# A hybrid decoder block on one core: the output projection and the second norm join the interleaved order of the mixers

## The chip, the core and the metric

The kernel runs on one core of a Trainium2 chip, whose engines each take their own instructions in order: TensorE (PE) for matrix products, VectorE (DVE), ScalarE (ACT) and GpSimd (POOL) for the rest, and SyncE (SP), whose queue starts most of the transfers. The metric is the device time of one execution in microseconds; lower is better. The granted clock is that of TensorE as a share of its full speed.

## What is computed

One decoder block for a sequence of 512 rows of width 1024. The part that the change touches, cut from the reference:

```python
h = rms_norm(x, norm1_w[l]) * (1.0 + scale1) + shift1
proj = h @ w_in[l]
aq, ak, av, gq, gk, gv, gg, glr = jnp.split(proj, split_points, axis=-1)
att = sliding_window_attention(aq..., ak..., av..., attn_sinks[l])
go = gla_chunked(gq..., gk..., gv..., log_a...)
go = rms_norm(go, gla_norm_w[l]).reshape(B, S, GLA_V_W) * jax.nn.silu(gg)
mixed = jnp.concatenate([att, go], axis=-1) @ w_out[l]
x = x + gate1 * mixed
h2 = rms_norm(x, norm2_w[l]) * (1.0 + scale2) + shift2
x = x + gate2 * peer_ffn(h2, peer_wq[l], peer_subkeys[l], peer_u[l], peer_v[l])
return rms_norm(x, final_norm_w)
```

The expert retrieval `peer_ffn` multiplies `h2` by `wq`, takes the best 16 keys twice, and works with rows of `u` and `v`; it makes up the time after about 258 us and its code is not touched.

## The kernel before

The 512 rows are four blocks of 128, `n` = 0 to 3. Products of float32 accuracy are made from two halves: a value is split into a high part (`hi`, `his`, `ah`, `gh`, `h2Th`, copied by ACT) and the rest (`lo`, `los`, `al`, `gl`, `h2Tl`, subtracted by DVE), and `mm3` (L119) adds three matmuls: high by high (L120), low by high (L121), high by low (L122).

Up to about 78 us the kernel computes the norm, the first modulations and narrow projections. Then comes a stretch in which five kinds of work are woven together by hand-written generators: the two wide products `pn` with `w_v` (`wide_load`, `wide_part`, tiles `wv..`; the results are `gv` and `gg`), attention (`sc` scores, `pt` transposes, `PT`, `po`), gated linear attention (`pa` scores of many tiny matmuls, `pd`, `go`), the sums of modulations 3 and 4 (`macc3`, `macc4`, then `mt3`, `mt4`, eight one-column matmuls each), and the gates. A class `Weave` decides the order: each step says which engine it needs, for how long by a written estimate, which places of a ring it takes and which marks must have been set, and the class gives the engine that is free first the step with the highest urgency. The order is then fixed for PE, ACT, DVE, SP and POOL alike (`manual_schedule`).

Behind that, outside the woven part, `mixers(n0)` runs for blocks 0 and 1 and then for 2 and 3, in an order that the framework's scheduler decides. For each half `q` of the 1024 columns it loads two pieces of 1 MB of `w_out` (`wo`), splits each in two parts (`his`, `los` of 128x1024, in a ring of four slots shared with the later splits of `wq` and `u`), and forms `pw` for two blocks. `mg` = `pw` times the gate (L1148), `x` + `mg` (L1149), the sum of squares (L1150). `second_norm` (L1154) takes the root (`rb..`), scales (`xs`, L1173 on ACT and L1175 on DVE), transposes (`x2t`, L1177), applies the modulation (`h`, L1181 on DVE, L1184 on ACT) and splits into `h2Th` (ACT, L1186) and `h2Tl` (DVE, L1187). Raw weights (`wo`, `wa` of the modulations, `wv`, `wq`, `u`) come through one pool of three slots of 1 MB, filled by SP's queue in order. Then `pq`, the products with `wq`, begin: `pq00` and `pq01` are the two halves of retrieval head 0, `pq10` and `pq11` those of head 1, first for blocks 0 and 1 (24 matmuls of 256 columns each), then, with the same names, for blocks 2 and 3; `qsc` copies the results.

## Time and profile before

| | |
|---|---|
| median of 3 runs | 1439.2 us (1437.43 to 1441.88) |
| the profiled execution | 1442.22 us, its span 1440.4 us |
| PE busy | 1396.3 us, 97% of the span |
| DVE busy | 1272.8 us, 88% |
| ACT busy | 669.0 us, 46% |
| POOL busy | 611.7 us, 42% |
| mean granted clock | 0.989 |
| HBM read | 399.71 MB |

The span is from the first to the last instruction, the time of the execution a little more. Busy time of an engine is the time in which an instruction of its own is being worked on; for PE the ends of matmuls are modelled, so its busy share says little of how fast it runs. "Idle before" is the time an engine stood still ahead of an instruction, and the name behind it is what ended last of the things waited for.

### The profile page before, as it was taken

How to read it: one execution, taken by the hardware profiler on the slowest of the kernel's cores; microseconds unless marked ns; L12 is line 12 of the kernel's file. 1: busy time of each engine (PE TensorE's matmuls, PEld its weight loads, DVE VectorE, ACT ScalarE, POOL GpSimd, SP SyncE). 2: the span in 40 equal slices, each digit the busy share in tenths (PEclk: the TensorE clock that was granted, in tenths of full speed). 3: DMA queues.
4: the chain of work that ended last, by engine and by line, in shares of the span. 5: the costliest groups of instructions: out<-in, count | busy, mean ns of one | idle time of the engine just before them, and what ended most of it. 6: DMA issues, size and time to landing. Idle time of an engine off the chain costs nothing.

```text
span 1440.4 us, 23298 instructions
## 1 busy us (share of the span) xinstructions
PE 1396.3 (97%) x8788; PEld 1229.5 (85%) x8788; DVE 1272.8 (88%) x2321; ACT 669.0 (46%) x1124; POOL 611.7 (42%) x400
## 2 busy tenths in 40 slices
PE   5999999999999999999989999999999999999997
PEld 4776687888999999999979888888888888888885
DVE  7778867589999999999978999999999898898996
ACT  4557566533344477766863333333233333323333
POOL 2000000144525444333035777677776776555510
PEclk9999999999999999999999999999999999999999
DMA  9621555353358999999889999999999999999962
GB/s 359 245 89 59 205 176 205 105 214 126 111 193 325 387 321 347 348 328 355 291 323 416 412 413 413 410 413 407 394 401 395 403 381 412 391 414 410 411 245 73
DMA packets 129985, 443.81 MB, mean 308 GB/s; under 512 B 11952, under 2 KB 48592, under 8 KB 109520
## 3 DMA queue, kind: packets, MB, share of 16 engines
q1 hardware_dynamic: 71136, 256.40, 47.0%
q0 software_dynamic: 47136, 171.99, 30.5%
q10 hardware_dynamic: 11600, 13.93, 2.7%
q8 instruction: 69, 1.13, 0.3%
q14 instruction: 44, 0.36, 0.1%
HBM read 399.71 MB, written 42.47 MB: 307 GB/s over the span
## 4 chain that ended last, share of the span: by engine, by line
PE 75%; DVE 10%; issue 6%; ACT 3%; DMA 3%; POOL 2%; SPq 0%; ACTq 0%; POOLq 0%; DVEq 0%
PE acc L122 12%; PE acc L120 12%; PE acc L121 12%; PE ph L122 8%; PE ph L120 8%; PE ph L121 8%; POOL spr L1542 2%; PE pg L1463 2%; PE pw L121 1%; PE pw L120 1%; PE pn L120 1%; DVE macc L282 1%; PE pw L122 1%; DMA u<-in_uT_dram 1%; PE pj L120 1%
## 5 line engine op out<-in xcount | busy, mean ns | idle before, releaser
L120 PE MATMUL ph<-h2Th,his 128*128 128x320 f32 x1024 | 320.1, 313 | 2.4 <-ACT his L1905 1.9
L122 PE MATMUL ph<-h2Th,los 128*128 128x320 f32 x1024 | 316.6, 310 | 2.5 <-DVE los L1912 1.8
L121 PE MATMUL ph<-h2Tl,his 128*128 128x320 f32 x1024 | 316.1, 309 | 0.0
L1598 POOL DMA_INDIRECT gu<-in_u_dram,ix_u x128 | 215.4, 1683 | 146.0 <-DVE gu L1608 81.1
L1633 POOL DMA_INDIRECT gv<-in_vP_dram,ix_v x128 | 212.8, 1662 | 111.4 <-DVE gacc L1638 88.4
L120 PEld LDWEIGHTS ph<-h2Th,his 128*128 128x128 f32 x1024 | 193.1, 189 | 4.3 <-ACT his L1905 2.1
L122 PEld LDWEIGHTS ph<-h2Th,los 128*128 128x128 f32 x1024 | 192.8, 189 | 3.5 <-DVE los L1912 2.0
L121 PEld LDWEIGHTS ph<-h2Tl,his 128*128 128x128 f32 x1024 | 193.1, 189 | 0.8
L1542 POOL DMA_INDIRECT spr<-in_u_dram,spix x64 | 104.7, 1636 | 171.5 <-DVE spr L1548 129.2
L120 PE MATMUL acc<-his,Ah 128*128 128x512 f32 x432 | 168.0, 389 | 0.0
L121 PE MATMUL acc<-los,Ah 128*128 128x512 f32 x432 | 168.0, 389 | 0.0
L122 PE MATMUL acc<-his,Al 128*128 128x512 f32 x432 | 168.0, 389 | 0.0
L1638 DVE SCALAR_TENSOR_TENSOR gacc<-gv,hg,gacc 128x1024 f32<-128x1024 f32 x127 | 162.6, 1280 | 2.1 <-DMA gv<-in_vP_dram,ix_v 1.8
L1608 DVE SCALAR_TENSOR_TENSOR gu<-gu,h2n 128x1024 f32<-128x1024 f32 x128 | 155.5, 1219 | 2.7 <-DMA gu<-in_u_dram,ix_u 2.7
L120 PE MATMUL acc<-hi,Ah 128*128 128x512 f32 x336 | 131.3, 391 | 0.0
L122 PE MATMUL acc<-hi,Al 128*128 128x512 f32 x336 | 131.1, 390 | 0.0
L121 PE MATMUL acc<-lo,Ah 128*128 128x512 f32 x336 | 130.7, 389 | 0.0
L1908 ACT ACTIVATE Ah<-gr 128x768 fp32r<-128x768 f32 x64 | 53.5, 836 | 134.5 <-PE acc L121 128.4
L113 ACT ACTIVATE his<-u 128x1024 fp32r<-128x1024 f32 x86 | 90.5, 1054 | 20.7 <-PE ph L121 9.5
L114 DVE TENSOR_TENSOR los<-u,his 128x1024 fp32r<-128x1024 f32 x75 | 91.4, 1222 | 8.6 <-ACT his L113 8.6
L121 PEld LDWEIGHTS acc<-los,Ah 128*128 128x128 f32 x432 | 81.1, 188 | 16.9
L120 PEld LDWEIGHTS acc<-his,Ah 128*128 128x128 f32 x432 | 81.1, 188 | 16.9
(697 smaller groups left out, 2899.8 us busy)
## 6 DMA issues: line engine op xcount, KB each, us to landing
u<-in_uT_dram SPq DMA_DIRECT2D x43, 1024.0 KB
gr<-Gd SPq DMA_DIRECT2D x15, 1536.0 KB
Gd<-gs SPq DMA_DIRECT2D x10, 2048.0 KB
gsp<-ge ACTq DMA_DIRECT2D x40, 320.0 KB
wa<-in_w_ada_dram SPq DMA_DIRECT2D x12, 1024.0 KB
wo<-in_w_out_dram SPq DMA_DIRECT2D x8, 1024.0 KB
wq<-in_wq_dram SPq DMA_DIRECT2D x8, 1024.0 KB
gp<-gsp SPq DMA_DIRECT2D x22, 320.0 KB
```

The lines of the kernel that those rows point to most:

```text
L113: nc.scalar.activation(hi, src, AF.Copy)
L114: lo_eng.tensor_tensor(lo, src, hi, OP.subtract)
L120: nc.tensor.matmul(acc, lh, rh, start=start, stop=False)
L121: nc.tensor.matmul(acc, lh, rl, start=False, stop=False)
L122: return nc.tensor.matmul(acc, ll, rh, start=False, stop=stop)
L1463: nc.tensor.matmul(pt[:, i, :], o12[:, g, 0, :, r], o2[:, g, m, :, r], start=(m == 0), stop=(m == 2))
L1542: nc.gpsimd.indirect_dma_start(out=sp[m], out_offset=None, in_=a["u"], in_offset=bass.IndirectOffsetOnAxis(ap=sp["ix", i][:, j:j + 1], axi ...
L1598: nc.gpsimd.indirect_dma_start(out=ur, out_offset=None, in_=a["u"], in_offset=bass.IndirectOffsetOnAxis(ap=ix_u[:, s:s + 1], axis=0))
L1608: nc.vector.scalar_tensor_tensor(ur, ur, 1.0, h2n, op0=OP.mult, op1=OP.mult, accum_out=hid[:, s:s + 1])
L1633: nc.gpsimd.indirect_dma_start(out=vr, out_offset=None, in_=a["vP"], in_offset=bass.IndirectOffsetOnAxis(ap=ix_v[:, s:s + 1], axis=0))
L1638: nc.vector.scalar_tensor_tensor(gacc, vr, hg[:, s:s + 1], gacc, op0=OP.mult, op1=OP.add)
L1908: nc.scalar.activation(grp(Ah), A, AF.Copy)
```

## The change

`Weave` and all its estimates go. The generators stay, each `yield` now only a place where a step begins, and a table `ORDER` of numbers says which generator takes its next step. The output projection and the second norm become generators of the same part: `pools` (opens the pools of the next stage and loads `x`), `out_load` (loads and splits `w_out` once, the first k row of the first half on its own), `project` (products `pw` of one half and one block), `joined`, `norm_root`, `norm_half`, `norm_end`. All four blocks of a half share the split, and eight PSUM banks take `pw`. `macc3` and `macc4` lie in the tile `Eg`, the transposes `gt` use other banks, and the loads of `wa` stand in another order. The ring of splits starts at 8 for `wq`.

```diff
-class Weave:
...
+ORDER = """
+2 2 2 2 0 0 0 0 2 0 0 0 0 22 2 2 25 25 0 0 2 25 21 25 0 2 25 25 13 13 13 25 2 0 1 13 1 1 2 1 1 1 1 25 2 1 13 1
...
+"""
...
+    def pools():
+        nonlocal h2p, h2Th, h2Tl, h2n, ix_u, ix_v, gg_g, hl, frW
+        yield
+        frA_s.close()
...
+        ring["slots"] = [hl.tile([P, 4, D], FR, name=name) for name in ("his", "los")]
+        yield
+        frT_s.close()
+        frW = frW_s.enter_context(tc.tile_pool(name="frW", bufs=1, side="right", reuse_waits="tile"))
+        for n in range(NT):
+            yield
...
+            nc.sync.dma_start(x1s[n], a["x"][n * P:(n + 1) * P, :])
+
+    def out_load():
+        for i in range(8):
+            q, k = divmod(2 * i, KD)
+            if i % 2 == 0:
+                yield
+                wo = raw([P, 4, 512], f"wo{q}{k}")
+                nc.sync.dma_start(wo, a["w_out"][:, k:k + 4, q * 512:(q + 1) * 512])
+            k0 = i % 2 * 2
...
+            yield
+            hi, lo = (t[:, i % 4].rearrange("p (a b) -> p a b", a=2)[:, :m] for t in ring["slots"])
+            nc.scalar.activation(hi, wo[:, k0:k0 + m, :], AF.Copy)
+            yield
+            nc.vector.tensor_tensor(lo, wo[:, k0:k0 + m, :], hi, OP.subtract)
...
+    def project(q, n, tag):
+        for k in range(KD):
+            yield
+            if k == 0:
+                pw[n, q] = pbank(f"pw{n}{q}") if tag == "ph" else bank(f"pw{n}{q}", tag)
+            h, l = [(ahl[n][i][:, k, :] if k < 4 else ghl[n][i][:, (k - 4) * P:(k - 3) * P]) for i in range(2)]
+            oh, ol = rows[q, k]
+            mm3(pw[n, q], h, l, oh, ol, k == 0, k == KD - 1)
...
+    def norm_half(n, half):
...
+        if half:
+            nc.scalar.activation(xs, x1s[n][:, 512:], AF.Copy, scale=h2s["r", n])
+        else:
+            nc.vector.tensor_scalar(xs, x1s[n][:, :512], h2s["r", n], None, op0=OP.mult)
...
+        for i in range(4):
+            nc.tensor.transpose(pt[:, i, :], xs[:, i * P:(i + 1) * P], ident)
...
+    def norm_end(n):
+        yield
...
+        nc.scalar.activation(h2Th[:, :, n * P:(n + 1) * P], h2s[n], AF.Copy)
+        yield
+        nc.vector.tensor_tensor(h2Tl[:, :, n * P:(n + 1) * P], h2s[n], h2Th[:, :, n * P:(n + 1) * P], OP.subtract)
...
+        parts = ([gla_scores(0), gla_scores(1), wide_load(0), wide_load(1), pools()] + [gla_gate(n) for n in ALL]
...
+                 + [project(0, n, t) for n, t in enumerate(("m", "m", "ph", "ph"))]
+                 + [project(1, n, t) for n, t in enumerate(("pt", "po", "m", "m"))]
+                 + [modulation(3), modulation(4)] + [attention_parts(n) for n in ALL])
+        for part in parts:
+            next(part)
+        for i in ORDER.split():
+            next(parts[int(i)], None)
...
+    hilo.n = 8
...
-    for n in range(0, NT, 2):
-        mixers(n)
```

PE at the start of the woven part, from the first product with `wv00` on; before:

```order
L120 MATMUL pn00_897<-wv00h_835,hTh_186 128x512
L121 MATMUL pn00_897<-wv00l_836,hTh_186 128x512
L122 MATMUL pn00_897<-wv00h_835,hTl_187 128x512
...
L798 MATMUL sc000_904<-am_128,identb_130 128x2x128
...
L884 MATMUL pa1_932<-Eg_113 64x64 x4
L891 MATMUL pa1_932<-Eg_113 64x32 x48
L120 MATMUL pn00_897<-wv02h_879,hTh_186 128x512
```

The same place after the change, from the k-step with which the first scores `sc` are now preceded (`wv02` is the third k-step, `pn01` the second block):

```order
L98 MATMUL pn00_897<-wv02h_829,hTl_187 128x512
L96 MATMUL pn01_898<-wv02h_829,hTh_186 128x512
L97 MATMUL pn01_898<-wv02l_830,hTh_186 128x512
L98 MATMUL pn01_898<-wv02h_829,hTl_187 128x512
...
L759 MATMUL sc000_932<-am_128,identb_130 128x2x128
...
L835 MATMUL pa1_946<-Eg_113 64x64 x4
L842 MATMUL pa1_946<-Eg_113 64x32 x48
L96 MATMUL pn01_898<-wv02h_829,hTh_186 128x512
```

Three k-steps of both blocks (18 matmuls) now stand ahead of `sc00`, where one of block 0 stood (3); 12 wide matmuls lead up to the `pa1` products before and 21 after.

PE where the projection ends, after the change: `pw31` and `pw21` are the second halves of blocks 3 and 2.

```order
L98 MATMUL pw31_2249<-his_1921,gl3_2137 128x512
L1009 MATMUL mt4_2310<-ones_79,Eg_113 128x1 x8
L96 MATMUL pw21_2326<-his_1921,ah2_1793 128x512
L97 MATMUL pw21_2326<-los_1922,ah2_1793 128x512
L98 MATMUL pw21_2326<-his_1921,al2_1792 128x512
L1131 MATMUL x2t0_2332<-ident_73,xs00_2299 128x128 x4
...
L98 MATMUL pw21_2326<-his_1921,gl2_2091 128x512
L1131 MATMUL x2t30_2411<-ident_73,xs30_2408 128x128 x4
L1131 MATMUL x2t31_2418<-ident_73,xs31_2398 128x128 x4
L96 MATMUL pq00_2510<-h2Th_1912,his_1921 128x256
L96 MATMUL pq01_2511<-h2Th_1912,his_1921 128x256
L97 MATMUL pq00_2510<-h2Tl_1913,his_1921 128x256
```

Before, `mt3` and `mt4` stood together ahead of the first `pw`, the transposes of blocks 0 and 1 stood before `pw21` and `pw31` began, and `pq00` followed the last `pw` with the transposes of blocks 2 and 3 behind it.

ACT and DVE at that place after the change, ACT first (from `h` of block 0's end; `h2_123` holds blocks 1 to 3):

```order
L1147 ACTIVATE h2_123_2356<-x2t10_2351,modT_83,aT_84 128x128 x2
L89 ACTIVATE his_1921<-wq0_2503 128x1024
L1154 ACTIVATE h2Th_1912<-h2_0_2337 128x8x128
L1147 ACTIVATE h2_123_2356<-x2t11_2361,modT_83,aT_84 128x128 x2
L89 ACTIVATE his_1921<-wq0_2503 128x1024
L1119 ACTIVATE xs31_2398<-x1_3_2234,rb3y_2339 128x512
L89 ACTIVATE his_1921<-wq1_2663 128x1024 x2
L1154 ACTIVATE h2Th_1912<-h2_123_2356 128x8x128
```

DVE:

```order
L1144 TENSOR_SCALAR h2_123_2356<-x2t11_2361,aT_84,modT_83 128x128 x2
L1121 TENSOR_SCALAR xs30_2408<-x1_3_2234,rb3y_2339 128x512
L1090 TENSOR_TENSOR mg21_2416<-pw21_2326,gate1b_102 128x512
L90 TENSOR_TENSOR los_1922<-wq0_2503,his_1921 128x1024
L90 TENSOR_TENSOR los_1922<-wq1_2663,his_1921 128x1024
L1092 TENSOR_TENSOR x1_2_2221<-x1_2_2221,mg21_2416 128x512
L90 TENSOR_TENSOR los_1922<-wq1_2663,his_1921 128x1024
L1156 TENSOR_TENSOR h2Tl_1913<-h2_123_2356,h2Th_1912 128x8x128
```

The split of `wq` (`his`, `los`) and the ends of the second norm of block 1 (`h2Th`, `h2Tl`) now alternate with the last steps of the projection (`mg21`, `x1_2`), where before `h2Th` and `h2Tl` of blocks 0 and 1 were finished ahead of the split of `wq`. From the first `pq` of blocks 2 and 3 on (the next `pq00` behind `pq11`), every engine has the order that it had.

## Rows read from the trace of the kernel before

**Rows 1.** The page: busy us of each engine (share of the span, instructions), and part 4, the chain of work that ended last, by engine.
```profile
PE 1396.3 (97%) x8788; PEld 1229.5 (85%) x8788; DVE 1272.8 (88%) x2321; ACT 669.0 (46%) x1124; POOL 611.7 (42%) x400
...
PE 75%; DVE 10%; issue 6%; ACT 3%; DMA 3%; POOL 2%; SPq 0%; ACTq 0%; POOLq 0%; DVEq 0%
```

**Rows 2.** The table of windows, from 78 us to the end of the output projection at 258.31 in one, and five of its pieces: length, busy time of each engine (instructions), granted clock of TensorE as a share of full speed, share of the DMA engines, GB/s.
```profile
core 0: us, PE busy (x) PEld busy (x) DVE busy (x) ACT busy (x) POOL busy (x), PEclk, DMA share, GB/s
78.00:258.31 180.31, 172.24 (x1293) 131.88 (x1292) 136.66 (x295) 114.11 (x253) 1.56 (x1) 0.95 0.41 141
78.00:100.00 22.00, 22.00 (x201) 17.69 (x201) 13.89 (x27) 14.03 (x13) 1.56 (x1) 1.00 0.14 49
100.00:120.00 20.00, 18.04 (x182) 12.75 (x179) 16.00 (x45) 11.23 (x34) 0.00 (x0) 0.83 0.32 107
120.00:140.00 20.00, 19.08 (x213) 12.69 (x212) 18.12 (x46) 16.54 (x39) 0.00 (x0) 1.00 0.12 41
...
200.00:220.00 20.00, 19.83 (x92) 16.64 (x92) 14.74 (x21) 14.78 (x20) 0.00 (x0) 0.83 0.32 106
240.00:260.00 20.00, 17.58 (x84) 14.35 (x82) 15.03 (x23) 12.16 (x20) 0.00 (x0) 0.91 0.39 129
```

**Rows 3.** The three longest waits of PE between 80 and 280 us: us in total, times, longest.
```profile
PE x2t L1177 <- ACT xs L1173: 2.0, 1, 2.0
PE pa L891 <- issue: 2.0, 1, 2.0
PE pn L120 <- ACT gv L774: 1.4, 1, 1.4
```

**Rows 4.** PE in order of time at the small products of the second GLA block (start, us, engine, line, operation, tiles, shapes, count; in brackets the idle time before and its releaser), and the window behind them (columns as in rows 2).
```profile
102.88 1.59 PE L891 MATMUL pa<-Eg 64*64 64x32 f32 x94
106.43 0.42 PE L891 MATMUL pa<-Eg 64*64 64x32 f32 x2 [1.96 <-issue]
...
106.00:114.00 8.00, 7.57 (x34) 5.27 (x35) 6.90 (x21) 3.51 (x13) 0.00 (x0) 0.59 0.27 79
```

**Rows 5.** PE at mt3 and mt4 with the window behind them, and at the mt of a later modulation with the window around it.
```profile
198.29 0.40 PE L122 MATMUL pn<-wv17h,hTl 128*128 128x512 f32 x1
198.53 4.24 PE L1080 MATMUL mt<-ones,macc 128*128 128x1 f32 x32
...
200.00:210.00 10.00, 9.83 (x46) 8.40 (x46) 8.17 (x11) 7.66 (x11) 0.00 (x0) 0.66 0.24 70
...
352.25 1.84 PE L273 MATMUL mt<-ones,macc 128*128 128x1 f32 x16
...
350.00:356.00 6.00, 6.00 (x36) 5.25 (x35) 6.00 (x44) 0.60 (x1) 3.42 (x4) 1.00 0.22 49
```

**Rows 6.** PE at the x2t transposes of blocks 0 and 1, the window around them, and the one behind.
```profile
244.08 1.09 PE L1177 MATMUL x2t<-ident,xs 128*128 128x128 f32 x8 [2.02 <-ACT xs L1173]
245.57 0.69 PE L120 MATMUL pw<-his,ah 128*128 128x512 f32 x1 [0.40 <-DVE mg L1148]
...
240.90:245.90 5.00, 2.58 (x17) 1.92 (x16) 3.51 (x7) 3.52 (x7) 0.00 (x0) 0.98 0.67 228
244.00:250.00 6.00, 5.52 (x20) 4.39 (x21) 4.77 (x11) 4.07 (x12) 0.00 (x0) 0.72 0.52 175
```

**Rows 7.** PE at the first products with wq (258.31 is also where the last matmul of the output projection hands over), and at the product from which the order is common; the windows of that whole stretch and of its 16 transposes of blocks 2 and 3.
```profile
258.31 0.28 PE L120 MATMUL pq<-h2Th,his 128*128 128x256 f32 x1
258.43 0.28 PE L121 MATMUL pq<-h2Tl,his 128*128 128x256 f32 x1
...
276.22 0.38 PE L120 MATMUL pq<-h2Th,his 128*128 128x256 f32 x1 [0.96 <-ACT qsc L1277]
...
258.31:276.22 17.91, 15.11 (x122) 13.86 (x120) 11.69 (x30) 11.38 (x25) 0.89 (x1) 1.00 0.59 188
263.97:268.45 4.48, 2.64 (x18) 1.68 (x16) 2.87 (x11) 3.39 (x8) 0.00 (x0) 1.00 0.83 255
```

**Rows 8.** Groups of instructions of DVE and ACT between 98 and 280 us (busy us, mean ns of one; idle before and releasers), the longest wait of the SP queue from 80 to 290, and two loads of 1 MB as they stand in the chain.
```profile
L114 DVE TENSOR_TENSOR los<-wo,his 128x1024 fp32r<-128x1024 f32 x16 | 19.1, 1223 | 9.4 <-ACT his L113 9.2
L1148 DVE TENSOR_TENSOR mg<-pw,gate1b 128x512 f32<-128x512 f32 x8 | 5.2, 685 | 0.9 <-PE pw L122 0.7 <-issue 0.2
...
L113 ACT ACTIVATE his<-wq 128x1024 fp32r<-128x1024 f32 x4 | 4.2, 1062 | 4.3 <-PE pw L122 4.3
L1186 ACT ACTIVATE h2Th<-h 128x1024 fp32r<-128x1024 f32 x4 | 4.0, 1053 | 0.0
L1184 ACT ACTIVATE h<-x2t,modT,aT 128x128 f32<-128x128 f32 x16 | 6.6, 454 | 2.5 <-PE x2t L1177 1.3 <-DVE h L1181 1.1
L1173 ACT ACTIVATE xs<-x,rb0y 128x512 f32<-128x512 f32 x1 | 0.7, 727 | 0.7 <-DVE rb0y L138 0.7
...
SPq L1139 <- DVE los L114: 33.3, 5, 14.6
...
304.15 5.34 DMA wa<-in_w_ada_dram
...
314.57 5.15 DMA wa<-in_w_ada_dram
```

**Rows 9.** DVE after the second norm, and the window from 400 to 505 us (columns as in rows 2).
```profile
281.73 1.23 DVE L114 TENSOR_TENSOR los<-u,his 128x1024 fp32r<-128x1024 f32 x1 [8.55 <-ACT his L113]
...
400.00:505.00 105.00, 105.00 (x721) 104.98 (x720) 102.82 (x225) 47.60 (x79) 41.72 (x31) 1.00 0.80 304
```

More of the change, by code (lines that the diff above doesn't have):

```diff
@@ L734, in wide_load @@
         for half in range(2):
-            yield need("DMA", 4.0 if g else 0.0, {"raw": 1}, [("w", 0, 7)] if g else [])
+            yield
             w = wide_raw(g, half) if g else wraw.pop(("wv", half))
@@ L738, in wide_load @@
                 k = 4 * half + j
-                yield need("ACT", 0.06 + 0.5 * n, {"hi": 1} if n == 2 else {"h32": 2})
+                yield
                 if n == 2:
@@ L843, in attention @@
             if hp + per == 4:
-                free("sS")
                 sS = None
-            yield need("ACT", 0.6, {"PT": 1})
+            yield
             PT = frT.tile([P, per, nh, P], F32, tag="PT", bufs=2, name=f"PT{n}{jj}{hp}")
             nc.scalar.activation(PT, pt, AF.Copy)
-            free("pt")
             pt = None
-            yield need("PE", 0.55, {} if jj or hp else {"po": 1}, [("po", n)] if jj and not hp else [])
+            yield
             if not (jj or hp):
@@ L885, in gla_scores @@
         for L in LW:
-            yield need("PE", 0.5, {}, after[1] if L > 3 else after[0])
+            yield
             lo = 64 + (L - 1) * 32
@@ L906, in gla_scores @@
             pb = None
-            free("m")
-            mark(("pd", i))
-        yield need("ACT", 0.42)
+        yield
         nc.scalar.activation(at[:64, :, 64:], pa[:64, :, :64], AF.Copy)
-        yield need("DVE", 2.5, {}, [("pd", n // 2)])
+        yield
         pd = pds[n // 2]
@@ L930, in gla_state @@
         off = n % 2 * 256
[L931 to L932 removed]
+        yield
         kl, qe, el = preps[n // 2]
@@ L999, in gla_gate @@
         pt = None
-        free("ph")
     def attention_parts(n):
-        yield need("ACT", 0.5, {}, [("mixA", n)] + ([("al", n - 1)] if n else []))
+        yield
         al = frG.tile([P, 4, P], FR, tag="mixA", bufs=NT + 1, name=f"al{n}")
@@ L1012, in second_prep @@
     def second_prep():
-        old = [("Spe", 0), ("Spe", 1), ("Dpe", 0)]
-        yield need("DVE", 1.0)
+        yield
         b = frG.tile([P, 512], F32, tag="b", bufs=1, name="b1")
@@ L1040, in second_prep @@
         for L in range(NL):
-            yield need("DVE", 0.9, {}, [("E", 3 if L < 4 else NL)])
+            yield
             m = 64 >> L
@@ L1075, in modulation @@
                 w = None
-                free("raw")
-        yield need("PE", 1.8, {"m": 1})
-        pb = bank(f"mt{v}")
+        yield
+        pb = bank(f"mt{v}", "pt")
         for i in range(KD):
@@ L1086, in modulation @@
         pb = None
-        free("m")
-        mark(("mod", v))
     def gates():
         for n, t in enumerate(gg):
-            yield need("ACT", 0.5 if n else 1.8, {}, [("pn", 1, m) for m in range(NT)], 2.0)
+            yield
             nc.scalar.activation(t, t, AF.Silu)
-            mark(("gg", n))
-        yield need("ACT", 1.3, {}, [("gl", NT - 1), ("al", NT - 1)])
+        yield
         nc.scalar.preload_act_table_set("natural_log_exp_and_others")
+    h2p = h2Th = h2Tl = h2n = ix_u = ix_v = gg_g = hl = frW = None
@@ L1108, in peer_block_kernel @@
-    for n in range(NT):
-        mixd[n] = [[t[:, k, :] for k in range(4)] + [u[:, k * P:(k + 1) * P] for k in range(4)]
-                   for t, u in zip(ahl[n], ghl[n])]
-    frA_s.close()
-    frT_s.close()
-    frW_s = ExitStack()
-    frW = frW_s.enter_context(tc.tile_pool(name="frW", bufs=1, side="right", reuse_waits="tile"))
-    h2p = ctx.enter_context(tc.tile_pool(name="h2p", bufs=1, side="left", reuse_waits="tile"))
-    h2Th = h2p.tile([P, KD, T], FR, name="h2Th")
-    h2Tl = h2p.tile([P, KD, T], FR, name="h2Tl")
@@ L1196, in peer_block_kernel @@
+        for part in parts:
+            next(part)
+        for i in ORDER.split():
+            next(parts[int(i)], None)
+        assert all(next(part, None) is None and part.gi_frame is None for part in parts)
+    hilo.n = 8
     gsp = dr.tile([P // 2, P, 2, TU], F32, name="gsp")
```

343 lines of the change are left out of this document (144 added, 199 removed), and 13 rows, old and new, of the table ORDER.

## The prediction, made before the changed kernel was run

> **What bounds the kernel now.** The page first: PE is busy 97% of the span and carries 75% of the chain of work that ended last, against 10% for DVE [rows 1]. A kernel in that state gets faster only where PE does nothing or runs at the lower clock, so the next view is the table of windows over the stretch that the change touches, 78 to 280 us [rows 2]. The reader is to see there two different losses. PE is busy for less than the window in several, for 172.24 of 180.31 us up to the end of the output projection. And the granted clock is 0.83, 0.83 and 0.91 in three windows, in which PE is busy yet does less. The waits of PE in that stretch name the first loss [rows 3]; narrower windows around each place show the second [rows 4 to 6].
>
> **What there is to gain.** I count only what lies before the last matmul of pw31, which ends the output projection at about 258.3 us [rows 7].
> - Idle time: 180.31 - 172.24 = 8.1 us [rows 2]. The largest pieces are 2.0 (x2t on xs), 2.0 (issue) and 1.4 (gv) [rows 3]. A recorded matmul of 512 columns lasts 0.40 us but its successor starts 0.24 later [rows 5], so idle time behind such a matmul is shown about 0.17 too short; seven of the stops stand behind one: +1.2.
> - Low clock: busy time times (1 - granted clock). 106 to 114 us: 7.57 x 0.41 = 3.1 [rows 4]. 200 to 210: 9.83 x 0.34 = 3.3 [rows 5]. 244 to 250: 5.52 x 0.28 = 1.6 [rows 6].
> Together 8.1 + 1.2 + 8.0 = **17.3 us**. Each low stretch follows a stretch in which PE was idle or did only tiny matmuls: 1.59 us of 64x32 products and 1.96 of idle [rows 4]; 4.24 us of the one-column mt3 and mt4 [rows 5]; 2.02 and 0.40 of idle among the x2t transposes [rows 6]. [...]
>
> **The change part by part.**
> *The set of matmuls is the same*, so nothing is taken from PE's work. From the first pq product of blocks 2 and 3 on (at 276.22 us [rows 7]) every engine keeps its order, so whatever is gained or lost before is handed on as a shift. DVE would not swallow it: it stands idle 8.55 us before its first los of u [rows 9], and in 400 to 505 us PE is busy for all of it [rows 9].
> *w_out loaded and split once.* Removed: four 1 MB loads; 16 his and 16 los become nine each, two of them half as long, so 8 x 1.05 = 8.4 us less on ACT and 8 x 1.22 = 9.8 on DVE [rows 8]. Price zero, since DVE is busy 14.74 and 15.03 of 20 us in two windows there and ACT 14.78 and 12.16 [rows 2]; PE covers them. If that cover were gone (DVE the last to arrive), it would be worth up to 8.4 to 9.8 us, but only out of the idle time already inside the 17.3.
> *The front of the order.* On PE 18 wide matmuls instead of 3 stand ahead of sc00, and 21 instead of 12 ahead of pa1. Before, PE ran through 94 tiny matmuls in 1.59 us and then stood still 1.96 with nothing that it waited for [rows 4]. With 9 x 0.23 = 2.1 us of wide work put ahead of the same rows, PE gets there 2.1 later while the program's position hardly moves; if the supply of instructions was late, the stop falls to about 0 and its low stretch with it. If it is tied to the tiny matmuls themselves, all stays: 1.96 + 3.1 = 5.1. For the first speaks that pa0, as many tiny matmuls, passed with PE busy 22.00 of 22 us [rows 2]. I take 0 and keep 5.1.
> [...] The row does not decide it: it shows 1.96 us ended by "issue", where nothing else that the trace records was late.
> *The middle.* Each PE wait of the old order is a consumer close behind its producer: gv 1.4, xs 2.0 [rows 3]. In the new order I walked PE along the rows' durations: wide products stand in between each time, and inputs are ready 0.2 to 1 us before PE comes. For a search with fixed costs such margins are thin; I leave **1.0 us** of new waits.
> *mt3 and mt4 are separated*, and 16 x2t transposes (x2t0, x2t1) now follow mt4 with only three pw matmuls between. mt3 alone: mt of modulation 5, 1.84 us inside dense products, did not lower the clock (1.00 in the window around it) [rows 5]; price 0. mt4 with transposes: 1.8 + 0.7 + 1.6 = 4.1 us, which is nearest to the old 4.24 us pair, so I take its whole low stretch, **3.3 us**; the low end is 0, by the mt5 row.
> *The loads.* wo and wa share three raw slots, and SP waits for their readers on DVE: 33.3 us in all before, 14.6 at longest [rows 8], without PE noticing. A 1 MB load then takes 5.2 us (5.34 and 5.15 in the chain) [rows 8]. In the new queue wo04 goes out when los<-wo00 frees its slot, needed some 7 us later; wo10 and wo14 land 2 to 10 before. Price 0; if a load is late, PE waits for all of the lateness. x1 loads wait on a pool that PE's po3 frees, but stand ahead of wo10 and wo14 in the queue, which is part of those margins.
> *The hand-over to wq speaks against the change.* Before, h2Th and h2Tl of blocks 0 and 1 were done long ago when pw ended, so pq00 started at once [rows 7]. Now pw21 is the last projection and reads all four ring slots till its end (call it T): its k1, k3, k5, k7 free them at T-4.1, T-2.8, T-1.4 and T (0.69 a k-step). ACT must pass through his of wq0 and wq1 (1.06 each), h2Th of block 0 (1.05), two h of block 1 (0.45 each) and xs31 (0.72) in the order printed above: wq0 first half -3.1, h2Th -2.0, h -1.1, wq0 second half -0.1, xs31 +0.6, wq1 halves +1.6 and +2.6, h2Th of block 1 +3.6 [rows 8]. DVE meanwhile, free of h of block 1 at about 0.0 (x1_2 is of the kind of mg, 0.69; h2Tl of the kind of los, 1.22; xs30 an estimate between them and nothing): xs30 +0.4, mg21 +1.1, los wq0 +2.3, los wq1 +3.4, x1_2 +4.1, los wq1 +5.2, h2Tl of block 1 **T+6.4**. PE's third pq product (pq00 with h2Tl) needs that. Up to there PE has 0.8 us of transposes and two small matmuls, so it stands still about 5.5 us after T in three pieces. Before, from the last pw matmul at 258.31 to the hand-over at 276.22 are 17.9 us with 96 x 0.12 + 24 x 0.1 = 13.9 of work, so 4.0 lost [rows 7]. Net **1.5 us** dearer. And 5.5 idle in 6.5 us is nearer to the stretch of rows 6 (2.4 idle in 5.0, then the clock fell, 1.6 lost) than to that of rows 7 (1.8 idle in 4.5, clock 1.00), so **1.6 us** for the clock; bounds 0 and 3.3.
> *Sum:* 17.3 - 0 - 1.0 - 3.3 - 1.5 - 1.6 = **9.9 us** gained. The profiled execution took 1442.2 us and would take 1432.3; it lies 3.0 above the median of 1439.2, against which I forecast **1429.3 us**.
>
> **The rivals.** (0.3%, 4.3 us, is about what a measurement here can tell from no change.)
> - *Best case:* the low clock after mt4 and after T does not come (3.3 + 1.6): gain 14.8, 1424.4. For it: mt5 and rows 7, where such stretches left the clock at 1.00. Against: three of the five stretches in rows 4 to 7 lowered it. 0.12.
> - *The issue gap stays with its low clock:* gain 4.8, 1434.4. For it: one cannot see a releaser. Against: pa0. 0.19, in which small extras push it within 0.3% in a third of the cases. [...]
> - *The shift is eaten at the hand-over:* DVE's chain from mg21 to h2Tl is longer than walked, by 4 us of split queued in front, with a low stretch of 3.3 instead of 1.6, so about 5.7 less: gain 4.2 or less, 1435 to 1439. For it: nine instructions of DVE and ACT in a strict row, each with a hop. Against: most have rows of their own. That the change does nothing, since PE is 97% busy already, would need the low-clock losses to come back elsewhere in equal size; it is in this case. 0.14.
> - *Slower:* raw slots shared by wo and wa run out. Each w_out load waits until DVE has read the previous user, and all three later loads are exposed: 3 x 5.2 = 15.6 of PE waiting, so 1439.2 - 9.9 + 15.6 = 1444.9. It decides from a lateness of 9.9 + 4.3 = 14.2 us on. For it: SP's 33.3 us of waiting, 14.6 in one piece [rows 8], and DVE busy for 18.12 of 20 us in one window [rows 2], which now becomes denser. Against: half of the loads are gone, and no wait of PE of over 1.4 us was on a split of w_out [rows 3]. 0.07.
> - *Forecast* as summed, gain 8 to 12: 0.48.
>
> **How the numbers follow.** Faster: 0.48 + 0.12 + two thirds of 0.19 + a little of 0.14 = 0.75. Same: the rest of these, 0.18. Slower 0.07. The range runs from the best case, a little beyond for the 1.0 of margins (1423.5), to the eaten hand-over's middle (1437.5); outside are the slower case and part of the one before. The forecast's own range is 1427 to 1431.5.
>
> **What would show it.** After: no idle of 1.96 near pa1 and granted clock 1.00 in 100 to 120; PE's waits before pw31 below 2 us in sum; last pw matmul near 245.4 us instead of 258.3 (17.3 - 1.0 - 3.3 earlier); behind it three waits, at x2t30, at the first pq00 and at the first pq00 with h2Tl, together 5 to 6 us, the last ended by DVE h2Tl; hand-over near 266 instead of 276; everything from there shifted and its waits unchanged. Wrong would be: a wait of PE on his or los of wo, behind which a DMA wo was late; a low clock in new places; or a shift at the hand-over that is gone by 400 us.

## The result, and the profile after

| | before | after |
|---|---|---|
| median | 1439.0 us (4 runs, 1437.43 to 1441.88) | 1428.2 us (4 runs, 1427.29 to 1431.14) |
| ratio | | 0.9926, 95% interval 0.9905 to 0.9948 |
| the profiled execution | 1442.22 us, span 1440.4 | 1427.29 us, span 1425.5 |

The kernel is 10.8 us faster, more than twice the 4.45 and 3.85 us by which the four runs of each kernel differ. The forecast was 1429.3 us. The two profiled executions differ by more, 14.9 us, and that difference matters below: the median agrees with the sum better than the sum's own terms do. Ratios and intervals leave out one execution on record, of the kernel with doubled splits below, which took 1731.8 us at a granted clock of 0.753.

The page after, parts 1 and 4, where [rows 1] showed PE with 75% of the chain and DVE with 10%:

```profile
PE 1385.7 (97%) x8788; PEld 1226.2 (86%) x8788; DVE 1262.3 (89%) x2314; ACT 659.4 (46%) x1117; POOL 611.6 (43%) x400
...
PE 88%; DVE 7%; DMA 3%; ACT 1%; issue 0%; ACTq 0%; SPq 0%; DVEq 0%
```

The same 8788 matmuls take 10.6 us less busy time, which points to a higher clock or tighter rows, and "issue" is gone from the chain. The table of windows after (columns as in [rows 2]): up to the last matmul of the output projection, at the old place of pa1, at the busiest stretch of DVE, and from the end of the output projection to the hand-over.

```profile
core 0: us, PE busy (x) PEld busy (x) DVE busy (x) ACT busy (x) POOL busy (x), PEclk, DMA share, GB/s
78.00:240.75 162.75, 162.43 (x1299) 127.64 (x1297) 125.57 (x293) 103.84 (x248) 1.30 (x1) 1.00 0.38 134
...
106.00:114.00 8.00, 8.00 (x137) 6.28 (x136) 6.21 (x23) 3.95 (x20) 0.00 (x0) 1.00 0.40 133
...
200.00:220.00 20.00, 20.00 (x95) 16.27 (x94) 18.71 (x21) 10.41 (x16) 0.00 (x0) 1.00 0.69 255
...
240.75:262.79 22.04, 16.26 (x122) 15.58 (x122) 14.02 (x27) 12.71 (x25) 1.86 (x2) 0.85 0.37 132
```

PE is busy for 162.43 of 162.75 us and the granted clock is 1.00 throughout, where it was 172.24 of 180.31 us at 0.95 [rows 2]. All that is lost now lies behind the last pw. The waits of PE from 80 to 280 us after (all but one of 0.3 us, at 98 us, ahead of the first product with `wv00`), to be read against [rows 3]:

```profile
PE pq L97 <- DVE h2Tl L1156: 2.9, 1, 2.9
PE x2t L1131 <- ACT his L89: 2.0, 1, 2.0
PE pq L96 <- ACT h2Th L1154: 0.8, 1, 0.8
```

PE in order of time after, at six places: the first product with `wv00`, pa1 and the product behind it, mt4 (whose tile is now `Eg`) and the x2t transposes of two blocks, the last pw (240.52), the three waits, and the product from which the order is common to both kernels (the *common product* below; reaching it is the *hand-over*).

```profile
100.36 0.48 PE L96 MATMUL pn<-wv00h,hTh 128*128 128x512 f32 x1
...
106.73 1.60 PE L842 MATMUL pa<-Eg 64*64 64x32 f32 x96
108.26 0.50 PE L96 MATMUL pn<-wv02h,hTh 128*128 128x512 f32 x1
...
231.69 1.84 PE L1009 MATMUL mt<-ones,Eg 128*128 128x1 f32 x16
...
234.18 1.91 PE L1131 MATMUL x2t<-ident,xs 128*128 128x128 f32 x16
...
240.52 0.40 PE L98 MATMUL pw<-his,gl 128*128 128x512 f32 x1
242.91 1.06 PE L1131 MATMUL x2t<-ident,xs 128*128 128x128 f32 x8 [1.99 <-ACT his L89]
244.82 0.79 PE L96 MATMUL pq<-h2Th,his 128*128 128x256 f32 x2 [0.84 <-ACT h2Th L1154]
248.56 0.58 PE L97 MATMUL pq<-h2Tl,his 128*128 128x256 f32 x1 [2.95 <-DVE h2Tl L1156]
...
262.79 0.28 PE L96 MATMUL pq<-h2Th,his 128*128 128x256 f32 x1
```

The name `his` at the first of the three waits is not what the transposes read. They read `xs`, whose last piece DVE finishes at 242.29 + 0.48 = 242.77 us, 0.14 before they start (the row of DVE is below); in the experiment with mt3 and mt4 together the distance is the same, 0.15 us, and there the row names DVE xs.

The last pw hands over at 240.52 + 0.23 = 240.75 us, the T of the prediction. From the first `wv00` product to T are 140.4 us. That product in the trace of before:

```profile
98.57 0.48 PE L120 MATMUL pn<-wv00h,hTh 128*128 128x512 f32 x1
```

Before, it was 258.31 - 98.57 = 159.7 us to the same point, T of that trace. From T to the common product are 22.0 us, before 17.9 [rows 7]. So 19.3 us are gained ahead of T and 4.1 given back behind it, 15.2 net. What follows the common product takes 1162.7 us instead of 1164.2: the gain is handed on. The start of the first `wv00` product itself lies 1.8 us later in this execution.

DVE behind T after; the h2Tl that PE's third pq product waits for is the last row:

```profile
239.38 1.22 DVE L90 TENSOR_TENSOR los<-wq,his 128x1024 fp32r<-128x1024 f32 x1
240.51 1.22 DVE L1156 TENSOR_TENSOR h2Tl<-h,h2Th 128x1024 fp32r<-128x1024 f32 x1
241.65 0.72 DVE L1144 TENSOR_SCALAR h<-x2t,aT,modT 128x128 f32<-128x128 f32 x2
242.29 0.48 DVE L1121 TENSOR_SCALAR xs<-x,rb3y 128x512 f32<-128x512 f32 x1
...
247.29 1.22 DVE L1156 TENSOR_TENSOR h2Tl<-h,h2Th 128x1024 fp32r<-128x1024 f32 x1
```

### The profile page after: what moved, and what is told of

It reads as the page before. It is cut to its first block, busy times and chain, and to the rows that moved or that the text cites. A ratio compares the mean times of both kernels' runs of the same rounds, so it can differ in the third digit from the quotient of the medians.

```text
span 1425.5 us, 23257 instructions
## 1 busy us (share of the span) xinstructions
PE 1385.7 (97%) x8788; PEld 1226.2 (86%) x8788; DVE 1262.3 (89%) x2314; ACT 659.4 (46%) x1117; POOL 611.6 (43%) x400
## 4 chain that ended last, share of the span: by engine, by line
PE 88%; DVE 7%; DMA 3%; ACT 1%; issue 0%; ACTq 0%; SPq 0%; DVEq 0%
PE acc L96 12%; PE acc L98 12%; PE acc L97 12%; PE ph L96 10%; PE ph L98 10%; PE ph L97 10%; PE pg L1452 5%; PE pn L96 1%; PE pn L98 1%; DMA wi<-in_w_in_dram 1%; PE pn L97 1%; PE pw L96 1%; PE pw L97 1%; PE pw L98 1%; PE pj L96 1%; PE pj L97 1%
## 5 line engine op out<-in xcount | busy, mean ns | idle before, releaser
L98 PEld LDWEIGHTS acc<-his,Al 128*128 128x128 f32 x432 | 81.1, 188 | 16.9
```

The costliest lines, as they stand in the source:

```text
L98: return nc.tensor.matmul(acc, ll, rh, start=False, stop=stop)
```

## The experiments

The stretch is given as two numbers read from PE's rows as above: from the first `wv00` product to T, and from T to the common product (in the trace of after 140.4 + 22.0). Medians are set against runs of the kernel before on the same chip.

**How much one trace is worth: both kernels again, unchanged.**

> The changed kernel unchanged, beside the three below on one chip. Expected as first measured, 1428.2 us (1427 to 1431). Its trace tells which parts of the first trace come again: PE waiting 2.0, 0.8 and 2.9 us behind the last pw matmul, and a stretch at the lower clock behind them. If the first trace was an odd one, the three waits differ by more than 0.5 us.

> The changed kernel unchanged, with a trace. Theory: 162 to 164 us from the first product to the hand-over (162.43 and 163.79 so far), the part before the last pw at 140.4 us again, with no stop and clock 1.00; what differs is the clock behind the last pw and what lies outside. Rival: the two traces so far are of fast executions (1427.3 and 1426.6 us, medians 1428.2 and 1429.1), and a slower one shows a stop or a low clock in the part before the last pw too, over 142 us.

> The kernel before unchanged, profiled once more, for the share of its first trace that belongs to that one execution. Expected: the same stop of 2.0 us at pa1 released by issue, the same three stretches at the lower clock, and 177 to 178 us from the first product with wv00 to the first wq product of blocks 2 and 3; a difference of over 1 us in that stretch means that the first trace was an odd one.

> The kernel before unchanged, once more with a trace. Its two traces so far are of executions at 1442.2 and 1443.8 us, both about 3 us above the median of 1439 to 1440. Theory: a median execution has the same waits and the same 2.0 us stop at PE's 600th record, and is shorter outside the stretch that the change touches: from the first product with wv00 to the hand-over 176 to 178 us as before (177.65 and 176.04), and the 3 us are in the start (first product at 98.6 or at 100.3 us) and in what follows the hand-over (1164.2 and 1165.6 us). Rival: the stop or the low clock behind it is shorter in a median execution, then the stretch takes 173 to 175 us and the loss that the change could remove was 2 to 3 us smaller than the ledger says.

> As the look before: theory 176 to 178 us from the first product to the hand-over and the rest of the difference outside; rival 173 to 175 us.

| run | time, us | to T | from T |
|---|---|---|---|
| after, again | 1429.1 median of 5 (ratio 0.9936, 0.9921 to 0.9950) | 140.4 | 23.4 |
| after, third trace | 1430.0 (one) | 140.4 | 23.4 |
| before, again | 1443.8 (one) | 158.1 | 17.9 |
| before, third trace | 1443.0 (one) | 158.4 | 17.9 |
| before, fourth trace | 1441.6 (one) | 155.1 | 17.9 |

The changed kernel repeats to 0.02 us ahead of T, in three traces. Behind T its three waits repeat too (2.0, 0.8 and 2.9), but the low clock that follows lasts longer in two of three (mean granted clock from T to the common product 0.78 in both, against 0.85). The kernel before doesn't repeat: in two of the three new traces the issue stop is there, in one it isn't. The third trace, PE in order of time at pa1:

```profile
104.81 1.59 PE L891 MATMUL pa<-Eg 64*64 64x32 f32 x94
108.67 0.30 PE L891 MATMUL pa<-Eg 64*64 64x32 f32 x2 [2.26 <-issue]
```

and the fourth, with the window around it:

```profile
104.40 1.60 PE L891 MATMUL pa<-Eg 64*64 64x32 f32 x96
105.93 0.50 PE L120 MATMUL pn<-wv02h,hTh 128*128 128x512 f32 x1
...
106.00:116.00 10.00, 9.13 (x52) 6.14 (x52) 9.15 (x30) 6.48 (x27) 0.00 (x0) 1.00 0.27 81
```

The same 96 tiny matmuls in the same program run straight through, and the clock stays at 1.00. So they cause neither the stop nor, by themselves, the low clock. Without the stop the stretch is 3.0 to 4.6 us shorter (155.1 against 158.1, 158.4 and 159.7). The rival named for these traces, 173 to 175 us up to the common product, is what the fourth shows (173.05), and that execution was nevertheless only 0.7 to 2.3 us shorter than the others: its part behind the common product took 1166.7 us, against 1164.2 to 1165.6. Taken together, the stretch from the first `wv00` product to the common product took 177.7, 176.0, 176.3 and 173.0 us before and 162.4, 163.8 and 163.8 after: a gain of 9.2 to 15.2 us by the pair chosen, 12.4 in the mean.

All four traced executions of before took 1441.6 to 1443.8 us, above every median of before measured here (1438.9 to 1440.4). Those of after took 1426.6 to 1430.0, around its medians (1428.2 and 1429.1). A typical execution of before is therefore 1 to 5 us shorter than those of which rows exist. That it is the stop which most of them lack would fit, in size and in what the next experiment shows; no row shows it, and it stays open. On record beside the doubled splits are 23 executions of before: eight with a mean granted clock up to 0.991 took 1440.7 to 1444.4 us, fifteen with 0.993 or more took 1436.8 to 1442.7. The clock is thus part of the difference, but it doesn't tell which executions had the stop: the traced ones with it have 0.989, 0.993 and 0.991, the one without it 0.993.

**Is the stop tied to the tiny matmuls or to a place in the program?** pa1 and the first scores `sc` are put back behind 12 and 3 wide products, as they stood before; the rest of the order is kept, in lines broken anew.

```diff
-2 2 2 2 0 0 0 0 2 0 0 0 0 22 2 2 25 25 0 0 2 25 21 25 0 2 25 25 13 13 13 25 2 0 1 13 1 1 2 1 1 1 1 25 2 1 13 1
+2 2 2 2 0 0 0 0 2 0 0 0 0 22 2 2 25 13 13 25 0 0 2 25 21 25 0 1 1 1 1 1 1 1 2 25 25 13 25 2 0 13 2 25 2 1 13 1
```

> Of the changed kernel only the front undone: sc00 behind the first k-step and pa1 behind 12 wide matmuls, in the order of the kernel before. Theory (the stop of 1.96 us belongs to that place in the order: a tight row of tiny matmuls comes before PE's supply has caught up): a stop of about 2 us with issue as its releaser comes again at the end of pa1, with a granted clock near 0.6 in the 8 us behind: 5 us more, 1433 us. Rival (the stop came from what else ran then, or by chance): no stop, clock 1.00, 1428 us within 1.

The median is 1429.0 us, ratio 0.9931 (0.9918 to 0.9945), against 1429.1 for after on the same chip: nothing is lost in the median. In the trace 1.4 us are lost up to T (141.8), half of them in the stop shown here. PE in order of time, with the window from the start of the span to just ahead of the stop:

```profile
103.19 1.60 PE L842 MATMUL pa<-Eg 64*64 64x32 f32 x96
...
106.15 0.50 PE L98 MATMUL pn<-wv02h,hTl 128*128 128x512 f32 x1 [0.70 <-issue]
...
0.00:106.10 106.10, 89.13 (x600) 69.36 (x600) 77.69 (x150) 54.67 (x88) 9.82 (x29) 1.00 0.63 235
```

The stop is back, at 0.70 us, but not inside pa1: it stands two wide products behind it. The count tells where: it comes after PE's 600th matmul and 600th weight load. In the traces of before with a stop, the count ahead of it is the same, for example in the third:

```profile
0.00:108.30 108.30, 90.03 (x600) 70.63 (x600) 80.34 (x156) 55.31 (x95) 10.04 (x29) 1.00 0.62 230
```

So the stop belongs to one place in the count of PE's records, as the prediction's first reading had it. In the first trace of before PE was there at 104.47 us [rows 4], 5.9 us behind the first `wv00` product, and went on at 7.9 (106.43). Here it was there at 6.4 us (106.15 - 0.70 - 99.09, the last the start of that product) and went on at 7.1. In after PE comes to that count within pa1, which lasts until 7.9 us behind the first product (108.26 - 100.36), and no stop is seen; nor is there one in the seven other traces of kernels with this front (the two repeats and the five experiments below). Where there is a stop, PE goes on 7.1 to 8.2 us behind the first product, as if something arrived then, and a PE that comes later doesn't notice. In the fourth trace of before PE was there after 5.8 us and did not stop, so it isn't always as late. The expectation of a full return with its low clock fell; a stop of 0.7 us didn't lower the clock (1.00 from 106 to 114 us). Over the whole span it is the only stop of PE with that releaser here and in the first two traces of before, and the trace of after has none. The cause isn't recorded and stays open.

**mt3 back in front of mt4.** The last two steps of modulation 3 (61) are moved to stand ahead of the last one of modulation 4 (62); the following lines of the table are only broken anew.

```diff
-61 11 19 26 20 26 61 28 26 19 26 11 28 11 19 20 11 19 26 26 19 61 53 26 12 26 61 4 28 19 12 54 28 61 20 28 12
-65 20 55 61 28 12 55 62 12 55 55 20 53 20 20 27 20 28 62 53 62 20 53 27 20 6 20 54 66 5 54 27 5 66 62 28 56 7 4
+61 11 19 26 20 26 61 28 26 19 26 11 28 11 19 20 11 19 26 26 19 61 53 26 12 26 61 4 28 19 12 54 28 20 28 12 65 20
+55 28 12 55 62 12 55 55 20 53 20 20 27 20 28 62 53 62 20 53 27 20 6 20 54 66 5 54 27 5 66 62 28 56 7 4 27 56 28
...
+58 60 49 48 60 47 49 60 50 47 60 29 50 29 60 29 50 60 60 30 34 29 33 30 60 30 61 61 62 52 36 30 52 52 59 62
```

> Of the changed kernel only mt3 moved, to stand directly ahead of mt4 as in the kernel before. Theory (a stretch of some 4 us in which PE does only tiny matmuls lowers the clock as an idle one does): the clock falls to about 0.66 in the 10 us behind, 3.3 us more, 1431.5 us. Rival (the stretch of the kernel before fell for another reason, the clock follows idle time alone): clock 1.00, 1428 us within 1.

The median is 1431.4 us, ratio 0.9953 (0.9940 to 0.9967), 2.3 above after on the same chip; up to T the trace loses 4.8 us (145.2). PE there, and the window:

```profile
229.85 1.84 PE L1009 MATMUL mt<-ones,Eg 128*128 128x1 f32 x16
231.94 2.53 PE L1009 MATMUL mt<-ones,Eg 128*128 128x1 f32 x16 [0.26 <-DVE modT L1012]
234.33 0.77 PE L96 MATMUL pw<-his,ah 128*128 128x512 f32 x1
...
235.76 3.62 PE L1131 MATMUL x2t<-ident,xs 128*128 128x128 f32 x16
...
230.00:242.00 12.00, 11.74 (x63) 10.74 (x62) 5.06 (x19) 5.15 (x13) 0.00 (x0) 0.72 0.11 44
```

With the pair together the clock falls, while the second mt is still running (2.53 us instead of 1.84), and the transposes behind it take 3.62 us instead of 1.91. Low clock costs 11.74 x 0.28 = 3.3 us here, the same as in the old kernel [rows 5]. In after, mt4 and 16 transposes stand in the same place, three wide products apart, and the clock stays at 1.00. In both falls mt3 and mt4 made one piece without wide work, 4.24 us [rows 5] and 4.5 us here (229.85 to 234.33, where the next pw starts, 0.26 of it a wait); two pieces of 1.84 and 1.91 us with 0.7 us of wide work between went without one. Whether the break made the difference, or that the second piece is transposes and not one-column products, no run separates. The intervals of the two medians overlap; the trace decides.

**Each split of w_out done twice.** This computes the same values; it puts back nearly the work that sharing removed, 8.0 us of ACT and 9.2 of DVE in eight instructions each. It puts it back on the way of every product, since `lo` now waits for `hi` twice over; the old order had its second splits for other blocks.

```diff
             nc.scalar.activation(hi, wo[:, k0:k0 + m, :], AF.Copy)
+            nc.scalar.activation(hi, wo[:, k0:k0 + m, :], AF.Copy)
...
             nc.vector.tensor_tensor(lo, wo[:, k0:k0 + m, :], hi, OP.subtract)
+            nc.vector.tensor_tensor(lo, wo[:, k0:k0 + m, :], hi, OP.subtract)
```

> Of the changed kernel the eight long splits of w_out done twice over (his and los written again with the same values): the work of 8 his and 8 los given back, 8.0 us of ACT and 9.2 of DVE, nothing else. Theory (sharing the split was worth nothing by itself, because PE covers it): 1429 us within 1, PE waits for los or his of wo below 1 us in sum. Rival (the new order has no room, each doubled split is late by about its own length and PE waits): 4 to 8 us of PE waits on los, 1433 to 1437 us, most of the gain gone.

The median is 1435.4 us, ratio 0.9964 (0.9951 to 0.9977). Against a ratio of 0.9926 to 0.9936 for after that is 4 to 5.5 us. Up to T the trace loses 7.3 us (147.7). A row of PE's waits and the window in which the clock fell:

```profile
PE pw L97 <- DVE los L1073: 3.2, 3, 1.3
...
200.00:210.00 10.00, 8.43 (x31) 5.83 (x30) 8.66 (x10) 7.64 (x10) 0.00 (x0) 0.83 0.19 51
```

PE stands still for 3.2 us on the splits, and behind two stops of 0.4 and 1.0 us among the gt transposes the clock is lower for a while (8.43 x 0.17 = 1.4 us). The time is in the range of the rival: in this order, at these places, there is no room for the work that sharing removed. How much of it an order made for unshared splits could have hidden is not shown, and the trace's 7.3 us are more than the medians say.

**Each load of w_out started twice.** The second transfer writes the same bytes into the same tile, so it waits until the first has landed: this makes each of four loads late, which is harsher than loading into other slots as before.

```diff
                 nc.sync.dma_start(wo, a["w_out"][:, k:k + 4, q * 512:(q + 1) * 512])
+                nc.sync.dma_start(wo, a["w_out"][:, k:k + 4, q * 512:(q + 1) * 512])
```

> Of the changed kernel each of the four loads of w_out started twice into the same place: the 4 MB given back, and each piece lands one transfer (about 5 us) later than it would. Theory (the pieces land 2 to 10 us before they are needed): at most one piece is late, by up to 3 us, 1429 to 1432 us, and PE's wait, if there is one, is released by his or los of wo. Rival (the loads were what bound the new order): every piece late, over 8 us of PE waits, above 1437 us.

The median is 1434.5 us, ratio 0.9963 (0.9951 to 0.9975), so 4 to 5 us more than after; up to T 4.0 more (144.4). The waits, of SP first and then of PE:

```profile
SPq L1057 <- DMA wo<-in_w_out_dram: 28.0, 4, 9.0
...
PE pw L96 <- ACT his L1070: 1.6, 1, 1.6
PE pw L97 <- DVE los L1072: 0.8, 1, 0.8
PE pw L98 <- DVE gl L938: 0.6, 1, 0.6
```

The second transfers wait 28 us in sum for the first; of that 1.6 and 0.8 us reach PE, at `his` and `los` of one and the same piece (222.6 and 223.9 us), while the 0.6 for `gl` is no wait for a load. One late piece is what was expected, but the time is above the expected 1429 to 1432 us. The clock stays at 1.00 behind the stops of 1.6 and 0.8 us (220 to 230 us). The loads have cover, and not enough for one more transfer each.

**The splits of wq ahead of the hand-over.** A generator for each half of `wq` puts its splits into the ring as steps of the table (67 and 68), and the last lines of the table are drawn up anew, so that h2Tl of block 1 needn't stand behind four splits. The products `pq` take these tiles instead of splitting anew, and the ring goes on at 12 instead of 8. The first lines of the table are kept.

```diff
+    def wq_split(h):
+        yield
+        fetch(a["wq"][h], h, 256, "wq")
+        r = wraw.pop(("wq", h))
+        early["wq", h] = []
+        for s in range(2):
+            yield
+            hi, lo = (t[:, 2 * h + s].rearrange("p (a b) -> p a b", a=4) for t in ring["slots"])
+            nc.scalar.activation(hi, r[:, 4 * s:4 * s + 4, :], AF.Copy)
+            yield
+            nc.vector.tensor_tensor(lo, r[:, 4 * s:4 * s + 4, :], hi, OP.subtract)
+            early["wq", h].append((hi, lo))
...
+67 68 58 49 58 48 60 49 48 60 47 49 60 50 47 60 29 50 29 62 60 29 62 50 60 30 34 29 33 30 60 30 36 35 30 33 34
+35 36 60 33 34 33 34 35 36 35 36 41 42 52 52 41 42 59 59 67 67 59 59 67 52 67 32 59 59 68 59 59 51 68 32 32 32
+68 51 40 39 68 51 39 40 31 39 40 31 39 40 31 31 37 38 37 38 37 38 37 38 44 43 44 43 44 44
```

> The hand-over with its chain taken away: mt4 in the middle of pw31, the transposes of blocks 0 and 1 before pw31 ends, and the splits of wq as steps of the table, behind h2Th and h2Tl of block 1 and in front of the work for blocks 2 and 3. Theory (PE stands still because h2Tl of block 1 is queued behind splits of wq that wait for ring places): the three waits of 5.8 us in sum shrink to below 1.5, the clock stays at 1.00 there, and the hand-over comes about 7 us earlier: 1421 us, ratio to before 0.988. Rival (DVE and ACT simply have too much work in these 10 us, in whatever order): the waits only move to the transposes of blocks 2 and 3 or to the pq products behind them, gain under 2 us: 1426.5 to 1428.5.

The median is 1426.1 us (1425.17 to 1428.39), ratio 0.9915 (0.9901 to 0.9928): the fastest kernel here, 3.0 below after on the same chip, though the intervals overlap a little. Up to T it takes the same 140.4 us; from T to the common product are 20.55 us. PE's waits and that stretch:

```profile
PE h2n L1177 <- DVE h L1160: 1.7, 1, 1.7
PE pq L96 <- ACT qsc L1282: 1.5, 1, 1.5
PE pq L96 <- ACT rb2y L1119: 1.3, 1, 1.3
PE pq L98 <- DVE los L718: 0.6, 1, 0.6
PE pq L97 <- DVE h2Tl L1172: 0.6, 1, 0.6
...
241.28:261.83 20.55, 14.91 (x122) 13.87 (x120) 14.20 (x31) 12.06 (x27) 0.12 (x1) 1.00 0.45 156
```

The three waits behind T shrink from 5.8 to 1.2 us and the clock stays at 1.00, so the place of the late h2Tl is confirmed. The 1421 us that this theory gave were not reached; the rival, that the waits only move, is nearer (1426.5 to 1428.5). Idle time of PE in the stretch is 5.6 us, nearly as in after (20.55 - 14.91, against 22.04 - 16.26): the waits moved to the norm of the other blocks and to `qsc`, in single pieces of at most 1.7 us with dense work between. What was won is the clock: PE is busy 1.35 us less with the same 122 matmuls.

**The same, with two splits on POOL.** If DVE's load were what makes the new waits, moving the splits of the second half of `wq` to GpSimd should remove them. The order was drawn up once more for it.

```diff
-            nc.vector.tensor_tensor(lo, r[:, 4 * s:4 * s + 4, :], hi, OP.subtract)
+            (nc.gpsimd if h else nc.vector).tensor_tensor(lo, r[:, 4 * s:4 * s + 4, :], hi, OP.subtract)
```

> As the kernel with wq's splits in the table, with the los of the second head's wq on POOL instead of DVE and with the root and scale of blocks 3 and 2 drawn forward. Theory (the rest of the hand-over's waits is DVE's amount of work: 20 us of DVE work for 20 us of time): 2.4 us less on DVE bring the waits behind T from 5.6 to about 3 and the time to 1424 us. Rival (the rest is set by PE's own place of the transposes of blocks 3 and 2 among the products, not by DVE): waits stay above 5, 1426 to 1428 us.

It isn't better: median 1429.7 us, ratio 0.9933 (0.9915 to 0.9950), 140.4 us up to T and 23.7 behind it. PE's longest stop there, and what DVE and POOL did ahead of it:

```profile
249.23 1.97 PE L1147 MATMUL x2t<-ident,xs 128*128 128x128 f32 x8 [2.51 <-DVE xs L1137]
...
243.12 2.30 DVE L1122 TENSOR_TENSOR rb3t<-rb3y 128x1 f32<-128x1 f32 x1
245.46 2.33 DVE L1123 TENSOR_TENSOR rb3t<-rb3t,rb3m 128x1 f32<-128x1 f32 x1
...
242.98 4.81 POOL L718 TENSOR_TENSOR los<-wq,his 128x1024 fp32r<-128x1024 f32 x2 [161.00 <-ACT his L716]
```

The same two lines in the run with all splits on DVE:

```profile
246.36 0.15 DVE L1122 TENSOR_TENSOR rb3t<-rb3y 128x1 f32<-128x1 f32 x1
246.55 0.16 DVE L1123 TENSOR_TENSOR rb3t<-rb3t,rb3m 128x1 f32<-128x1 f32 x1
```

The `xs` for which the transposes wait comes late, and the clock falls behind them (8 transposes in 1.97 us against 1.06; the granted clock is 0.79 from 250 to 264 us). It is late because two steps of the root of block 3, one column each, take 2.30 and 2.33 us on DVE instead of 0.15 and 0.16, in just the time in which POOL works on its two `los` (242.98 to 247.79): each takes about as long as one of them. That puts some 4.3 us into the chain to `xs`, more than the stop of 2.51. DVE lost two splits and was busy longer behind T, 16.30 us against 14.20. So the run doesn't tell whether DVE's load makes the waits: what the move took from DVE came back, and more. That POOL's work is what holds DVE is inferred from these times, in this one trace, and not shown.

## Why the prediction was right, and where it was not

The forecast median was met within 1.1 us. The mechanism, PE's idle time and low clock ahead of T taken away and part of the gain given back at the hand-over, is the one that the traces show. Its terms were not all met, and part of the agreement is luck.

- *What there is to gain, 17.3 us ahead of T:* right in kind, and nearly all was gained. PE's idle time up to T went from 8.1 to 0.3 us and no low clock is left. The traces give 19.3, 2.0 more than the ledger; its low clock (8.0) was summed from three windows only, while the mean of 0.95 over 172.24 us allows 8.6 and, with its rounding, up to 9.5. The rest of the 2.0 has no row. Against the other traces of before the gain ahead of T is 14.7 to 18.0.
- *Front of the order, stop taken as 0 and 5.1 kept:* right for the traces, in three of three no stop; the clock is 1.00 from 106 to 114 us. The reason, that PE comes later to the same place of its program and that the tiny matmuls are not the cause, is borne out by the 600 records and by the trace in which the same pa1 runs through; what arrives late was not seen. The price of 5.1 is not borne out: with the old front put back the stop was 0.7 us, 1.4 us were lost in the trace and nothing in the median. What the prediction could not know from one trace is that the stop isn't in every execution of before.
- *mt4 with the transposes, 3.3 lost:* wrong, and the mis-sized term: it measured 0. The step chose the nearest row by the sum (4.1 us against 4.24), as if the 0.7 us of wide products between counted with the tiny work. The low end, 0 by the mt5 row, was the right one: the two pieces, 1.84 and 1.91 us, did not act as one. The pair put together again brought the 3.3 back.
- *The middle, 1.0 for thin margins:* it measured 0, no wait of PE at all between 100 and 240 us. The margins are thin nevertheless: with the doubled splits or the late loads, 3.0 to 3.6 us of waits stand there at once.
- *Price zero for sharing, "PE covers them":* not so in the order as it is now, as far as splits doubled in place can show it. In the old order DVE was busy 14.74 of 20 us in that part [rows 2]; in the new one 18.71. The cover that the prediction named was that of the old order, and the new order used it up. It had bounded the case (worth up to 8.4 to 9.8 us, out of the 17.3) and then chosen the end that didn't hold: it was 4 to 5.5 us by the medians. Since the 17.3 were counted whole, the sum didn't suffer by it.
- *Hand-over, 1.5 + 1.6:* the mechanism was right, with three waits at the three places named, 5.8 us in sum (5.5 forecast), the last ended by h2Tl. It was later than walked, 248.51 - 240.75 = T+7.8 instead of T+6.4: DVE had h2Tl of block 0 and two h of block 1 still ahead of it, and reached xs30 at T+1.5 where the walk had it at T+0.0; from there on the walk holds, 6.2 us for its 6.4 (the durations that it names add up to 6.7). By the prediction's product the clock lost 16.26 x 0.15 = 2.4 us here, but the same 122 matmuls were busy 15.11 us at 1.00 before [rows 7], so 1.2 by busy time; the rest of the 4.1 is idle time, 5.8 against 2.8. In the other two traces the clock lost more (0.78 over 23.4 us, against 0.85 over 22.0). Together 4.1 to 5.5 instead of 3.1.
- *Last pw near 245.4, hand-over near 266:* 240.75 and 262.79, the first by the terms above. What comes behind was handed on, as forecast.

Between the two first traces the gain was thus 15.2 and not 9.9 us, near the rival "best case" (14.8) though by another split: its low clock after T did come. The median shows 10.8 because the profiled execution of before was 3.2 above its median (3.0 above the one that the prediction knew) and that of after 0.9 below. The forecast of the median subtracted a sum made on an execution 3.0 us above the median from the median itself. Had the sum been exact, the forecast would have been 1424, 4 us too low. If a typical execution of before lacks the stop, its ledger is 3.0 to 4.6 us shorter and this is explained; without a trace of a typical execution, that is argued and not shown. Over all seven traces the gain is 12.4, between the forecast and this pair. Of the other rivals, the eaten hand-over came in part (1.0 to 2.4 us beyond the forecast, where the rival had 5.7), and the loads and raw slots of the slower case never showed in PE's waits (ACT stood 2.1 us for one load of `w_out`).

## What to carry to other kernels

When an order is drawn up anew, price a removed instruction by the slack of the new order, not by the busy share of the old: splits of `w_out` made PE wait 0.2, 1.1 and 0.5 us in the first, second and fourth trace of the old one, and the same work put back into the new one cost 4 to 5.5 us. Look for low clock behind unbroken stretches of tiny matmuls or idle time (0.66 behind 4.24 us of mt3 and mt4, 0.55 from 244 to 250 us among the three stops behind T), and try to break them with dense work before removing anything: with 0.7 us of wide products between mt4 and the transposes the clock stayed at 1.00, though no run separates the break from the kind of the second piece. Before work is moved to an engine with time to spare, look at what runs beside it: beside two splits on POOL two one-column steps of DVE took 4.3 us longer. And take a second trace before a loss with no releaser goes into a ledger: here it was absent in one execution of four.
